# Strassen forms for the gate projection's sixth unit and for the attention half's up-projection, doubled products beside plain units, and x loaded by GpSimd's queue

## The chip, the cores and the metric

One core of one Trainium2 chip runs the whole layer in one launch. The metric is device time in microseconds (us), the median of the runs. The kernel before took 2658.71 us, the median of 3 runs that lie between 2658.05 and 2658.91.

## The reference

The inputs are x, 512 tokens of 2048 features, per-layer embeddings p of 256 features, and the weights. All of it is float32.

```
h   = RMSNorm(x)
[u | v_sgu | q | k | v_att | g_a | g_b] = h @ W_in
y_a = u * (tril(W_s) v_norm + b)            # 8 groups, chunks of 128 tokens
y_b = stick_breaking_attention(q, k, v_att) # 8 heads of 128
x  += (sigmoid(g_a) * (y_a W_up_a) + sigmoid(g_b) * (y_b W_up_b)) @ W_o
x  += SwiGLU(RMSNorm(x))                    # hidden size 5632
x  += sigmoid(RMSNorm(x) @ W_pg) * (p @ W_ple)
```

Here u and v_sgu go through GELU, and q, k and v_sgu have an RMSNorm over each group of 128. W_in has 9216 columns, of which g_a and g_b are 2048 each.

## The kernel before, in words

**Precision.** A float32 operand is split into a high part, which TensorE takes as fp32r, and the low rest. A product is three matmuls, high by high, high by low and low by high (`mm3`, L296 to L298).

**Units and pairs.** Everything is transposed: features on the partitions, tokens along the row. One output tile is a *pair*, 256 output features by 512 tokens. It is summed over *units*, each of 256 inputs by 256 outputs. A *plain* unit ("P") is four blocks of weights with three matmuls of 512 columns each, 12 in all. A *Strassen* unit ("S") needs seven products of half the columns (`PRODUCTS`), 21 matmuls of 256 columns. A product can be *doubled* (L692): its high weights meet high and low of the other operand in one matmul of 512 columns, with one matmul of 256 for the low weights. With `doubled=5` an S unit has 16 matmuls, with 7 it has 14. A doubled product holds a PSUM bank of its own until VectorE and ScalarE have added its halves (`mix_doubled`, L751). There are six banks in the pool "ps" and two in the pool "small"; y and z are the names of the two banks that the last two products, and all plain units, sum into. A pair that mixes S and P units is not doubled.

**Forms.** The operand that isn't weights is kept as *forms*: high and low blocks, four for a plain form, seven for S. A form that comes late starts as a plain one, with part of its blocks, and gets its other blocks by a second load of its source (`late_form`). The tables `..._UNTIL` say for how many of the first pairs each unit is used plain.

**Weights.** SyncE (SP) issues the loads of the weights in a planned order (L339 for P, L341 and L343 for S). For S, GpSimd (POOL) adds two blocks to two others on their way by an accumulating DMA (L363), which waits until the base has landed and stands in order with GpSimd's other work. ScalarE then writes the high parts `whi` (L359), VectorE two sums (L375) and the low parts `wlo` (L356), into three slots. There are four landing buffers.

**Order of work.** PE works through the pairs in a written order, and between units a clock ticks. `after(n, fn)` puts a step n ticks later, and `beside(steps)` runs a generator step by step, where `yield n` waits n ticks. `finish_waiting()` runs all that still waits at once.

**Stages in order.** First the embedding product (`ple_pair`), while x's eight tiles are loaded (`load_x`, L899). Then the projection with `w_in`: three plain pairs, whose weights are named `w_first`, and 33 more; the pairs of g_a and g_b are spilled to DRAM (`gsp`). Four pairs "s" feed the spatial gating in `sgu_v`: it transposes a tile on PE (L1029), norms it (ScalarE's L1052 with `rr`, which GpSimd works out at L928), and multiplies with W_s on PE (L1214, into the bank `mp`). The up-projection has 16 pairs of four plain units, in the order b, a for each j (b is the attention half with y_b, which was spilled; a the gating half with y_a). With each comes a reload of the gate, its scaling by the norm's row (`scaled`, L1224), the sigmoid and the merge. Then w_o (S, seven doubled), FFN in (S, seven doubled), FFN out in three passes, and the gate projection with eight pairs of five S units and three P units, undoubled. In its last pair `finish` (L1457 to L1469) closes pieces of the output as they come ready.

## Time and profile before

| what | us |
|---|---|
| median of 3 runs | 2658.71 |
| profiled execution, its own time | 2659.74 |
| its span | 2658.0 |
| PE busy (TensorE's matmuls) | 2638.2, 99% |
| VectorE busy | 2234.6, 84% |
| ScalarE busy | 1403.2, 53% |
| GpSimd busy | 448.1, 17% |

| stage, from the span's start | us |
|---|---|
| embedding product | 5.08 to 16.14 |
| first three projection pairs | 16.14 to 86.31 |
| the other 33 projection pairs | 86.31 to 815.28 |
| up-projection | 815.28 to 1004.59 |
| w_o | 1004.59 to 1165.98 |
| FFN in | 1165.98 to 2031.82 |
| FFN out | 2031.82 to 2481.78 |
| gate projection, and the end | 2481.78 to 2658.0 |

A stage begins with its first matmul. The records of the stages can be cut further at each pair's first matmul, which gives the price of one pair. A row of the view by windows lists a stretch (start:end), its length, then for PE, PE's weight loads, VectorE, ScalarE and GpSimd the busy time with the number of instructions, then the granted clock of TensorE (1.00 is full speed), the share of the DMA engines and GB/s. A row of the waits names an engine and its line, the engine and line that released it, the total wait, how often, and the longest. In a timeline, what stands in brackets is the idle time before an instruction and who ended it.

### The profile page before, as it was taken

The page shows a single profiled execution, that of the slowest core. Times are in us where ns is not written, and L with a number is a line of the kernel's source. Part 1 is how long each engine was busy: PE and PEld are TensorE (multiplying, and loading weights), DVE is VectorE, ACT ScalarE, POOL GpSimd, SP SyncE. Part 2 cuts the span into 40 slices and gives each one's busy share as a digit, 9 for nine tenths or more (in the row PEclk, how much of TensorE's full clock was granted, in tenths as well). Part 3 has the DMA queues.
Part 4 walks back from the last instruction along what each step waited for, and adds up shares of the span by engine and source line. Part 5 has one row for each costly group of instructions (what it writes and reads, how often), then busy time and mean ns, then how long its engine had stood idle before and what let it go on. Part 6 is the DMA issues. An engine that isn't in the chain of part 4 may idle for free.

```text
span 2658.0 us, 42554 instructions
## 1 busy us (share of the span) xinstructions
PE 2638.2 (99%) x15336; PEld 2312.3 (87%) x15336; DVE 2234.6 (84%) x3821; ACT 1403.2 (53%) x2233; POOL 448.1 (17%) x556
## 2 busy tenths in 40 slices
PE   8999999999999999999999999999999999999999
PEld 7888888888998888888888888888888888889898
DVE  8687878787886558999888888888889989989876
ACT  7756565655554334566444444444445445455543
POOL 0122222232220001101111111111110211211110
PEclk9999999999999999999999999999999999999999
DMA  7677777777775668978888888788887989978884
GB/s 229 162 194 171 192 173 191 172 191 179 178 191 183 232 212 268 265 236 218 223 210 216 206 200 203 194 209 204 199 207 221 257 227 273 229 229 260 256 240 123
DMA packets 293459, 559.77 MB, mean 211 GB/s; under 512 B 26368, under 2 KB 140544, under 8 KB 293248
## 3 DMA queue, kind: packets, MB, share of 16 engines
q1 hardware_dynamic: 231136, 441.95, 50.7%
q0 software_dynamic: 62112, 115.11, 27.5%
q8 instruction: 120, 1.97, 0.3%
q14 instruction: 91, 0.75, 0.1%
HBM read 505.57 MB, written 51.38 MB: 210 GB/s over the span
## 4 chain that ended last, share of the span: by engine, by line
PE 90%; DVE 4%; DMA 3%; issue 1%; ACT 1%; SPq 0%; POOL 0%; ACTq 0%; POOLq 0%; DVEq 0%
PE ps L692 53%; PE ps L298 10%; PE ps L297 9%; PE ps L296 9%; PE small L692 6%; DVE wlo L356 1%; DVE wholes L527 1%; DMA wholes<-w_ffn_out 1%; PE small L1103 1%; PE small L1155 1%; DVE parts L287 1%; PE small L1029 1%; DMA x<-wholes 1%; ACT whi L359 0%; PE small L1214 0%
## 5 line engine op out<-in xcount | busy, mean ns | idle before, releaser
L692 PE MATMUL ps<-parts,whi 128*128 128x512 f32 x4200 | 1409.4, 398 | 1.6 <-DVE out L796 1.0
L359 ACT ACTIVATE whi<-wholes 128x512 fp32r<-128x512 f32 (+2 forms) x940 | 871.5, 941 | 745.8 <-DVE wholes L375 286.6
L356 DVE TENSOR_TENSOR wlo<-wholes,whi 128x512 fp32r<-128x512 f32 (+2 forms) x940 | 979.4, 1076 | 73.7 <-ACT whi L359 73.0
L692 PEld LDWEIGHTS ps<-parts,wlo 128*128 128x128 f32 x4200 | 790.2, 188 | 178.2 <-issue 1.9
L692 PE MATMUL ps<-parts,wlo 128*128 128x256 f32 x4200 | 831.3, 279 | 0.9 <-DVE wlo L356 0.9
L692 PEld LDWEIGHTS ps<-parts,whi 128*128 128x128 f32 x4200 | 677.1, 189 | 10.5 <-issue 3.6
L297 PE MATMUL ps<-parts,whi 128*128 128x256 f32 (+1 forms) x1832 | 605.0, 331 | 0.7 <-DVE parts L287 0.5
L298 PE MATMUL ps<-parts,wlo 128*128 128x256 f32 (+1 forms) x1832 | 604.9, 331 | 0.5 <-DVE wlo L356 0.5
L296 PE MATMUL ps<-parts,whi 128*128 128x256 f32 (+1 forms) x1816 | 597.3, 330 | 7.4 <-ACT parts L286 5.3
L297 PEld LDWEIGHTS ps<-parts,whi 128*128 128x128 f32 x1832 | 347.0, 189 | 39.0 <-DVE parts L287 2.7
L296 PEld LDWEIGHTS ps<-parts,whi 128*128 128x128 f32 x1816 | 343.6, 190 | 40.4 <-ACT parts L286 5.7
L298 PEld LDWEIGHTS ps<-parts,wlo 128*128 128x128 f32 x1832 | 347.3, 190 | 32.4 <-DVE wlo L356 1.6
L375 DVE TENSOR_TENSOR wholes<-wholes 128x256 f32<-128x256 f32 (+1 forms) x820 | 345.0, 421 | 17.9 <-DVE wlo L356 1.4
L751 DVE TENSOR_TENSOR out<-out,ps 128x256 f32<-128x256 f32 x490 | 202.3, 416 | 147.6 <-ACT out L748 147.4
L363 POOL DMA_DIRECT2D wholes<-w_ffn_in x169 | 147.1, 870 | 702.1 <-DVE wholes L375 251.7
L363 POOL DMA_DIRECT2D wholes<-w_in x132 | 116.6, 885 | 531.3 <-DVE wholes L375 132.8
L692 PE MATMUL small<-parts,whi 128*128 128x512 f32 x480 | 190.3, 397 | 0.0
L287 DVE TENSOR_TENSOR parts<-wholes,parts 128x1024 fp32r<-128x1024 f32 (+3 forms) x137 | 122.8, 907 | 18.5 <-ACT parts L286 18.5
L286 ACT ACTIVATE parts<-wholes 128x1024 fp32r<-128x1024 f32 (+3 forms) x137 | 106.5, 800 | 54.2 <-DVE wholes L527 35.7
L748 ACT ACTIVATE out<-ps 128x256 f32<-128x256 f32 x258 | 96.3, 383 | 50.7 <-PE ps L692 46.7
L363 POOL DMA_DIRECT2D wholes<-w_ffn_out x64 | 55.7, 871 | 360.6 <-DMA wholes<-w_ffn_out 89.2
L1402 ACT ACTIVATE out<-out 128x512 f32<-128x512 f32 x44 | 27.9, 633 | 155.6 <-DVE out L1401 155.6
(124 smaller groups left out, 1770.0 us busy)
## 6 DMA issues: line engine op xcount, KB each, us to landing
wholes<-w_ffn_in SPq DMA_DIRECT2D x169, 384.0 KB, 5.5
wholes<-w_in SPq DMA_DIRECT2D x132, 384.0 KB, 5.1
wholes<-w_ffn_in SPq DMA_DIRECT2D x169, 256.0 KB, 4.7
wholes<-w_ffn_in POOLq DMA_DIRECT2D x169, 256.0 KB, 5.3
wholes<-w_in SPq DMA_DIRECT2D x132, 256.0 KB, 4.3
wholes<-w_in POOLq DMA_DIRECT2D x132, 256.0 KB, 5.0
wholes<-w_ffn_out SPq DMA_DIRECT2D x64, 384.0 KB, 6.3
wholes<-x SPq DMA_DIRECT2D x45, 512.0 KB, 5.8
```

The source lines that it names most:

```text
L286: return (nc.scalar.activation(hi, src, AF.Copy), nc.vector.tensor_tensor(out=lo, in0=src, in1=hi.bitcast(F32), op=ALU.subtract))
L287: nc.vector.tensor_tensor(out=lo, in0=src, in1=hi.bitcast(F32), op=ALU.subtract))
L296: nc.tensor.matmul(ps, sh, mh, start=start, stop=False)
L297: nc.tensor.matmul(ps, sh, ml, start=False, stop=False)
L298: return nc.tensor.matmul(ps, sl, mh, start=False, stop=stop)
L356: in_turn(nc.vector.tensor_tensor(out=self.lo[:, blocks], in0=r, in1=h.bitcast(F32), op=ALU.subtract))
L359: in_turn(nc.scalar.activation(h, r, AF.Copy))
L363: nc.gpsimd.dma_start(out=raw[:, 3:5], in_=self.src[:, 1:3], accum_op=ALU.add)
L375: in_turn(nc.vector.tensor_tensor(out=o, in0=x, in1=y, op=ALU.add))
L692: m = nc.tensor.matmul(out, l, r, start=first and k == 0, stop=last and k == 1)
L748: in_turn(nc.scalar.activation(out, x, AF.Copy, scale=scale))
L751: in_turn(nc.vector.tensor_tensor(out=out, in0=x, in1=y, op=op))
```

## The change

Four things change.

1. **Gate projection.** `GATE` goes from five S and three P units to six and two; the sixth is S from j = 2 on. All its pairs get `doubled=5` although they still hold plain units: five products take five "ps" banks, y takes the sixth, and z goes to a "small" bank. The plain units then start the bank z themselves.
2. **Up-projection of the attention half.** The four units of `w_up_b` become S, undoubled, with late forms for y_b: none at j = 0, two at j = 1, all four from j = 2 on, 26 unit uses in all. For j = 0 the order becomes a, b.
3. **Start.** x's tiles from the third on are issued by GpSimd instead of SP, p's first half by ScalarE, and ScalarE's table load comes behind that.
4. **Around the gating and the up-projection.** `sgu_v` waits three ticks rather than two before W_s's matmuls. `finish_waiting()` between projection and up-projection goes; what waits is carried over. The scaling of the 16 gates by the norm's row moves into the projection, two ticks after each gate pair and ahead of its spill; the sigmoid comes two ticks after its load rather than one.

The diff:

```diff
@@ -30,11 +30,12 @@
 EPS = 1e-6
 MASKED = -1e4
 
+UP_UNTIL = 1, 1, 2, 2
 PASSES = "SSSSSSSS", "SSSSSSSS", "SSSSPP"
 HALF = 1, 1, 1, 1, 2, 2, 2, 2
 PLAIN_UNTIL = HALF, HALF, (2, 2, 2, 2, 1, 1)
-GATE = "SSSSSPPP"
-GATE_UNTIL = 1, 1, 2, 2, 2, 1, 1, 1
+GATE = "SSSSSSPP"
+GATE_UNTIL = 1, 1, 2, 2, 2, 2, 1, 1
 PLACE = 7 * 256
 LATER = 3
 FFN_UNTIL = 1, 1, 2, 2, 2, 2, 2, 2
@@ -611,8 +612,10 @@
                     src, far)
 
     def plain_form(src, ready=always, gain=None, raw=1024, how="low", far=False):
+        hows = [how] * 2 if isinstance(how, str) else how
+
         def steps(form):
-            hi, lo = form.blocks = parts.take(1024, how), parts.take(1024, how)
+            hi, lo = form.blocks = [parts.take(1024, h) for h in hows]
             w = form.raw()
             if gain:
                 gained(hi.own(), w.f(), *gain)
@@ -629,7 +632,7 @@
             return tuple([x.own(0, T), x.own(T)] for x in form.blocks)
             yield
 
-        return Form("P", steps, [(parts, 1024, how)] * 2 + [(wholes, raw, "low")] * bool(raw),
+        return Form("P", steps, [(parts, 1024, h) for h in hows] + [(wholes, raw, "low")] * bool(raw),
                     ready, src, far)
 
     class Pair:
@@ -643,12 +646,13 @@
             self.n = {k: kinds.count(k) for k in "SP"}
             self.left = dict(self.n)
             self.both = all(self.n.values())
-            self.doubled = 0 if self.n["P"] else doubled
+            self.doubled = 0 if self.n["P"] and doubled > 5 else doubled
             self.o, self.home, self.banks = None, home, {}
 
         def at(self, name):
             if name not in self.banks:
-                self.banks[name] = small_bank() if name == len(PRODUCTS) - 1 else bank()
+                small = "z" if self.both and self.doubled else len(PRODUCTS) - 1
+                self.banks[name] = small_bank() if name == small else bank()
             return self.banks[name]
 
         def ends(self):
@@ -666,10 +670,11 @@
                     for ps, bs in zip(self.ends(), ((3, 2), (1, 0))):
                         for k, b in enumerate(bs):
                             first = start and u + k == 0
+                            fresh = not self.both or (self.doubled > 0 and b < 2)
 
                             mark(mm3(ps, wh[:, b], wl[:, b], xh[k], xl[k],
-                                     first and not self.both, stop and u == n - 1 and k == 1,
-                                     first and self.both and b < 2))
+                                     first and fresh, stop and u == n - 1 and k == 1,
+                                     first and not fresh and b < 2))
                     if prepare and u == 0:
                         prepare_late()
                     tick()
@@ -777,7 +782,8 @@
                 tt(c12, c12, p3[1], add)
             else:
                 yield
-                tt(o[:, :T], self.at("y"), o[:, :T], sub)
+                if not self.both:
+                    tt(o[:, :T], self.at("y"), o[:, :T], sub)
             yield
 
         def out(self, o=None):
@@ -842,11 +848,10 @@
             for u, ((xh, xl), (wh, wl)) in enumerate(ws):
                 for k, i in enumerate(bs):
                     mm3(ps, wh[:, i], wl[:, i], xh[k][:, a:b], xl[k][:, a:b],
-                        c + a > T and u + k == 0, k == 1 and u == len(ws) - 1)
+                        c + a >= T + (p.doubled == 0) and u + k == 0, k == 1 and u == len(ws) - 1)
             done(p.o, c + a, c + b, ps)
 
 
-    nc.scalar.preload_act_table_set("natural_log_exp_and_others")
 
     more_landings(4)
     for i in range(3):
@@ -858,11 +863,13 @@
     ple_spill = {}
     ps_p = []
 
-    def ple_operands():
+    def ple_operands(queue=None):
         raw = take(1024, "old")
         ps_p.extend(parts.take(1024, "high") for _ in range(2))
         for k in (0, T):
-            nc.sync.dma_start(out=raw.f(k, k + T), in_=pT[:, k : k + T])
+            (queue or nc.sync).dma_start(out=raw.f(k, k + T), in_=pT[:, k : k + T])
+            queue = None
+        for k in (0, T):
             split_into(*(x.own(k, k + T) for x in ps_p), raw.f(k, k + T))
         give(raw)
 
@@ -896,10 +903,12 @@
 
     def load_x():
         x_raw.append(take(1024, "old"))
-        nc.sync.dma_start(out=x_raw[-1].f(), in_=xT[len(x_raw) - 1])
+        queue = nc.gpsimd if len(x_raw) > 2 else nc.sync
+        queue.dma_start(out=x_raw[-1].f(), in_=xT[len(x_raw) - 1])
 
     w_ple_0 = plain_weights(w_ple[0])
-    ple_operands()
+    ple_operands(nc.scalar)
+    nc.scalar.preload_act_table_set("natural_log_exp_and_others")
     ple_pair(0, w_ple_0)
     load_x()
     gcol = consts.tile([P, ng], F32, name="gcol")
@@ -1207,7 +1216,7 @@
             rr = power(ssq, NT)
             yield 1
             times(gv, ps, rr)
-            yield 2
+            yield 3
             mp = small_bank()
             for t in range(NT):
                 s = slice(t * P, (t + 1) * P)
@@ -1218,6 +1227,10 @@
                 scalar=gcol[:, g_sgu + g : g_sgu + g + 1],
                 in1=bb.unsqueeze(1).to_broadcast([P, NT, P]),
                 op0=ALU.mult, op1=ALU.add)
+        if rnd == 3:
+            assert ("b", 3) in y_done
+            give(*att.values())
+            att.clear()
 
     def scaled(o, row):
         b = o.rearrange("p (b t) -> p b t", t=T)
@@ -1273,8 +1286,9 @@
 
     def plan_rest():
         for j in range(KU):
-            for b in "ba":
-                plan((w_up_a if b == "a" else w_up_b)[j], "PPPP")
+            for b in "ba" if j else "ab":
+                plan((w_up_a if b == "a" else w_up_b)[j],
+                     "PPPP" if b == "a" else now("SSSS", UP_UNTIL, j))
             if 0 < j < 6:
                 planned.append((w_ple[j + 2].rearrange("p (b c) -> p b c", b=4), 1, "P"))
         for j in range(KU):
@@ -1290,11 +1304,14 @@
             plan(w_gate[j], now(GATE, GATE_UNTIL, j))
 
     def y_form(c, i):
-        return plain_form((lambda: y_a[i]) if c == "a" else lambda: load(y_spill[i]),
-                          lambda: len(y_done) == 8, raw=0 if c == "a" else 1024,
-                          far=c == "b")
-
-    ys = {(c, i): y_form(c, i) for c in "ba" for i in range(4)}
+        def ready():
+            return len(y_done) == 8
+
+        if c == "a":
+            return plain_form(lambda: y_a[i], ready, raw=0, how="low" if i else ("high", "low"))
+        return late_form(lambda size=1024: load(y_spill[i], size), ready, far=True)
+
+    ys = {(c, i): y_form(c, i) for c in "ab" for i in range(4)}
     build(ys.values())
     for n, ((w, i), pr) in enumerate(zip(order, made())):
         if n == 0:
@@ -1323,11 +1340,14 @@
             nc.vector.tensor_tensor(out=y_a[i].f(), in0=o, in1=y_a[i].f(), op=ALU.mult)
             y_done["a", i] = True
         else:
-            d = tc.dram_tile([P, 1024], F32, name=nm("gsp"))
-            nc.sync.dma_start(out=d, in_=o)
-            gate_spill[w, i] = d
-    finish_waiting()
-    give(*att.values())
+            d = gate_spill[w, i] = tc.dram_tile([P, 1024], F32, name=nm("gsp"))
+
+            def spill_gate(o=o, d=d):
+                scaled(o, row1)
+                nc.sync.dma_start(out=d, in_=o)
+
+            after(2, spill_gate)
+    after(3, lambda: give(norm1.block))
 
 
     part = {}
@@ -1348,19 +1368,18 @@
     ms = [spilled_form("S", "mix", j) for j in range(KU)]
     build(ms)
     for j in range(KU):
-        for b in "ba":
+        for b in "ba" if j else "ab":
             s = load(gate_spill[b, j], 1024, "low")
             g = s.f()
-
-            def gate(g=g):
-                scaled(g, row1)
-                nc.scalar.activation(g, g, AF.Sigmoid)
-
-            after(1, gate)
-            pr = pair([ys[b, i] for i in range(4)], last=j == KU - 1)
-            for h, ps in zip((g[:, :T], g[:, T:]), pr.ends()):
-                nc.vector.tensor_tensor(out=h, in0=h, in1=ps, op=ALU.mult)
-            if b == "b":
+            after(2, lambda g=g: nc.scalar.activation(g, g, AF.Sigmoid))
+            pr = pair([ys[b, i] for i in range(4)], last=j == KU - 1, j=j,
+                      until=UP_UNTIL if b == "b" else None)
+            if pr.n["S"]:
+                tt(g, g, pr.out(), ALU.mult)
+            else:
+                for h, ps in zip((g[:, :T], g[:, T:]), pr.ends()):
+                    tt(h, h, ps, ALU.mult)
+            if j not in part:
                 part[j] = s
             else:
                 nc.vector.tensor_tensor(out=g, in0=g, in1=part[j].f(), op=ALU.add)
@@ -1372,8 +1391,6 @@
             ple_pair(j + 2)
             if j == 5:
                 ple_done()
-    give(norm1.block)
-
 
     norm2 = Norm()
     fs = [spilled_form("S", "x1", j, (g_ffn, j)) for j in range(KU)]
@@ -1476,9 +1493,9 @@
         if j:
             after(LATER, rest)
         if j == KU - 1:
-            pair(gs, j=j, until=GATE_UNTIL, parts_done=finish)
+            pair(gs, j=j, until=GATE_UNTIL, parts_done=finish, doubled=5)
         else:
-            o = pair(gs, j=j, until=GATE_UNTIL).out()
+            o = pair(gs, j=j, until=GATE_UNTIL, doubled=5).out()
             if j:
                 close(o)
             else:
```

What the change moves, at three places. First SP's queue at the start of the program (`ple` are stores of the embedding product, `w_first` the weights of the first three projection pairs, `xT` the tiles of x). Before:

```order
L339 DMA wholes<-w_first 128x512
L899 DMA wholes<-xT 128x1024 x2
L884 DMA ple_110<-out_91 128x1024
L339 DMA wholes<-w_first 128x512
L884 DMA ple_157<-out_140 128x1024
L899 DMA wholes<-xT 128x1024
L884 DMA ple_179<-out_162 128x1024
L339 DMA wholes<-w_first 128x512 x3
```

Now:

```order
L340 DMA wholes<-w_first 128x512
L907 DMA wholes<-xT 128x1024
L340 DMA wholes<-w_first 128x512 x3
L891 DMA ple_110<-out_91 128x1024
L340 DMA wholes<-w_first 128x512
L891 DMA ple_157<-out_140 128x1024
L340 DMA wholes<-w_first 128x512
L891 DMA ple_179<-out_162 128x1024
L342 DMA wholes<-w_in 128x2x256 x2
```

Three more loads of `w_first` stand ahead of the first store, whose source is only there when the first embedding pair is done. GpSimd's queue, now, at the same place:

```order
masks.py:197 MEMSET ident 128x128
L907 DMA wholes<-xT 128x1024
masks.py:199 ISA
masks.py:199 AFFINE_SELECT ident<-ident 128x128
L924 AFFINE_SELECT tri<-ones 128x128
L907 DMA wholes<-xT 128x1024
L364 DMA wholes<-w_in 128x512 x2
L907 DMA wholes<-xT 128x1024
```

Before, none of the rows on `xT` stood there; the third tile of x is now the second thing that GpSimd does in the program.

Second PE in a late pair of the gate projection, where its last S unit ends and the next plain unit begins (`ps_...` and `small_...` are banks of PSUM, `whi` and `wlo` weights). Before:

```order
L298 MATMUL ps_23817<-parts,wlo_81 128x256
L296 MATMUL ps_23824<-parts,whi_80 128x256
L297 MATMUL ps_23824<-parts,whi_80 128x256
L298 MATMUL ps_23824<-parts,wlo_81 128x256
...
L296 MATMUL ps_23824<-parts,whi_78 128x512
L297 MATMUL ps_23824<-parts,whi_78 128x512
L298 MATMUL ps_23824<-parts,wlo_79 128x512
```

Now:

```order
L697 MATMUL ps_24014<-parts,whi_75 128x512
L697 MATMUL ps_24014<-parts,wlo_76 128x256 x2
L697 MATMUL ps_24014<-parts,whi_75 128x512
L297 MATMUL ps_24019<-parts,whi_75 128x256
L298 MATMUL ps_24019<-parts,whi_75 128x256
L299 MATMUL ps_24019<-parts,wlo_76 128x256
...
L299 MATMUL ps_24019<-parts,wlo_80 128x512
L297 MATMUL small_24128<-parts,whi_79 128x512
L298 MATMUL small_24128<-parts,whi_79 128x512
L299 MATMUL small_24128<-parts,wlo_80 128x512
```

The products ahead of y are doubled now, and the plain units sum into y's bank and into a small bank.

Third PE around W_s's matmuls of the spatial gating (L1214 before, L1223 now). Before:

```order
L297 MATMUL ps_6402<-parts,whi_78 128x256
L298 MATMUL ps_6402<-parts,wlo_79 128x256
L1214 MATMUL small_6515<-wholes 128x128 x4
L692 MATMUL ps_6368<-parts,whi_76 128x512
L692 MATMUL ps_6368<-parts,wlo_77 128x256 x2
```

Now:

```order
L299 MATMUL ps_6416<-parts,wlo_78 128x256
L697 MATMUL ps_6382<-parts,whi_75 128x512
L697 MATMUL ps_6382<-parts,wlo_76 128x256 x2
...
L697 MATMUL ps_6403<-parts,whi_75 128x512
L697 MATMUL ps_6403<-parts,wlo_76 128x256 x2
L697 MATMUL ps_6403<-parts,whi_75 128x512
L1223 MATMUL small_6565<-wholes 128x128 x4
```

One group of doubled products, which stood behind W_s's four matmuls, now stands ahead of them.

## The prediction

> **What bounds the kernel now.** I read the page's busy times first, then PE's waits, then windows cut at the first matmul of each pair.
>
> ```profile
> PE 2638.2 (99%) x15336; PEld 2312.3 (87%) x15336; DVE 2234.6 (84%) x3821; ACT 1403.2 (53%) x2233; POOL 448.1 (17%) x556
> ```
>
> PE is busy for 2638.2 of 2658.0 us. So there are two ways to a shorter time: fewer columns through PE, or fewer of the some 20 us in which it is idle. The waits of PE (engine and line, who released it, total, times, longest) show the second:
>
> ```profile
> PE small L1214 <- ACT wholes L1052: 2.2, 1, 2.2
> PE ps L296 <- ACT whi L359: 2.1, 2, 1.9
> PE ps L692 <- DVE out L796: 1.0, 2, 0.8
> ```
>
> None is large, and all but the 1.0 lie at places that the change touches. The rest of the idle time is the head and the tail of the program.
>
> **The price of a unit.** Windows of five pairs: an up-projection pair (four plain units), w_o's second (four plain, four S undoubled), a late gate pair (five S undoubled, three plain), a projection pair of eight S doubled five times, and an FFN pair doubled seven times.
>
> ```profile
> 887.63:898.51 10.88, 10.88 (x50) 9.02 (x49) 6.23 (x7) 3.96 (x6) 0.00 (x0) 1.00 0.64 223
> 1026.35:1047.36 21.01, 21.01 (x134) 19.14 (x133) 19.31 (x35) 12.71 (x16) 2.65 (x3) 1.00 0.89 263
> 2548.26:2569.07 20.81, 20.81 (x143) 19.41 (x142) 15.23 (x24) 8.59 (x11) 3.00 (x3) 1.00 0.84 226
> 602.88:622.66 19.78, 19.78 (x130) 17.97 (x129) 15.63 (x27) 8.72 (x13) 3.49 (x4) 1.00 0.84 215
> 1270.28:1289.81 19.53, 19.53 (x114) 17.05 (x112) 17.30 (x32) 9.37 (x14) 4.33 (x5) 1.00 0.93 229
> ```
>
> PE's busy time equals the length in each, so these are prices of work. Plain: 10.88 / 4 = 2.72. S undoubled: (21.01 - 10.88) / 4 = 2.53, and from the gate pair (20.81 - 3 x 2.72) / 5 = 2.53 again. S doubled five times: 19.78 / 8 = 2.47.
>
> **Up-projection.** 26 unit uses go from 2.72 to 2.53: 26 x 0.19 = **-4.9**. What each b pair adds on other engines (S weights by accumulating DMA, VectorE's two sums and more low parts, the mixing) is about half of what eight S units need in the 602.88 row: 15.6 / 2 = 7.8 us of VectorE and 8.7 / 2 = 4.4 of ScalarE in a pair of 10.12, so PE's work hides it; without that cover it would cost the excess. The second halves of y_b's forms must be there for j = 1, about 11 us after j = 0's start; the w_o pair above does the same in its row without idle PE. Bound: nothing to 1.5, the idle time of w_o's third pair here, whose two waits for L796 are the 1.0 above:
>
> ```profile
> 1047.36:1069.83 22.47, 21.50 (x122) 18.27 (x121) 19.75 (x35) 11.67 (x16) 3.82 (x5) 1.00 0.98 283
> ```
>
> (22.47 against 21.01.) I take nothing, since the nearer row (1026.35) has no wait. The scaling of the gates moves from here into the projection: 16 x 1.22 us of VectorE, where it is busy for 15.63 of 19.78, so it fits. The DMA that spills each gate moves behind it by two ticks; its reload comes hundreds of us later.
>
> **Gate projection.** Six unit uses go from 2.72 to 2.47, 6 x 0.25 = -1.5, and the 32 S uses that exist (2 at j = 1, 5 at j = 2 to 7) get doubled, 32 x 0.06 = -1.8: **-3.3**. VectorE's share rises: from 15.23 by one S unit's share of the 602.88 row (15.63 / 8 = 1.95, less a plain unit's 6.23 / 4 = 1.56) and by the mixing of five doubled banks, at most the difference between FFN's 17.30 and 15.23: some 17.8 of 20.3. FFN's 17.30 of 19.53 is the same share, and PE waits for nothing there. In the last pair the end is set by y:
>
> ```profile
> 2648.41 0.69 DVE L1457 TENSOR_TENSOR out<-ps,out 128x512 f32<-128x512 f32 x1 [2.46 <-PE ps L298]
> ...
> 2653.73 1.45 DVE L1469 TENSOR_TENSOR out<-out,wholes 128x256 f32<-128x256 f32 x3
> ```
>
> From y's last matmul VectorE runs a chain to 2655.18. Behind y's last product stood 36 matmuls of 256 columns; now there are 24, so y ends 12 x 0.12 later relative to the pair's end and, with the pair 0.5 shorter, 0.8 later than before, with less work behind it. I give back 0.6 of the gain, bounds 0 and 0.8: **-2.7**.
>
> **The gating's wait.** The pair in which PE waited, then the stretches around the wait, and the chain of waits through it:
>
> ```profile
> 622.66:648.20 25.54, 23.31 (x146) 21.13 (x145) 18.01 (x31) 13.73 (x27) 4.91 (x6) 0.93 0.68 158
> ...
> 637.80:640.57 2.77, 0.54 (x5) 0.33 (x3) 0.00 (x0) 0.67 (x3) 1.94 (x2) 1.00 0.86 210
> 640.57:643.98 3.41, 3.41 (x15) 3.12 (x15) 0.78 (x2) 2.01 (x4) 0.92 (x1) 0.50 0.75 115
> ```
>
> ```profile
> 631.78 5.48 DMA wholes<-w_in
> ...
> 637.93 0.86 POOL wholes L363
> 638.79 1.08 POOL rr L928
> 639.87 0.02 issue
> 639.90 0.38 ACT wholes L1052
> 640.27 0.04 issue
> 640.32 1.69 PE small L1214 x7
> ```
>
> The small `rr` stood on GpSimd behind an accumulating DMA that waited for a load of weights, ScalarE's L1052 for `rr`, and PE for that: 2.2 us idle, then 3.41 us at a clock of 0.50. The pair took 25.54, where its neighbour with the same extra work took 21.43:
>
> ```profile
> 581.45:602.88 21.43, 21.43 (x135) 18.92 (x133) 15.99 (x27) 9.27 (x14) 3.48 (x4) 1.00 0.79 222
> ```
>
> So the place costs 4.1. The changed order puts eight products of 512 columns and as many of 256 between: 8 x 0.227 + 8 x 0.12 = 2.7 us more work ahead of W_s's matmuls, against 2.2 idle. It is enough by 0.5, and the clock isn't lowered: **-3.9**, bounds 0 and -4.2.
>
> The Trainium skill, page "TensorE: Matmul & The Clock Gate", section "HAM oscillation — how this bites in real kernels", tells to leave no gap on PE over some 3.4 us. The trace differs: 2.2 us were followed by a row at 0.50. By the page alone only the 2.2 of idle time would come back, and the sum below would be 1.7 smaller in its gain; the measurement decides.
>
> **Entry of the up-projection.** Its first two pairs, of the same plain units:
>
> ```profile
> 815.28:826.85 11.57, 11.35 (x51) 8.76 (x49) 8.95 (x13) 7.37 (x8) 0.00 (x0) 1.00 0.76 232
> 826.85:838.67 11.82, 11.29 (x49) 9.04 (x50) 10.59 (x11) 6.97 (x8) 0.00 (x0) 1.00 0.46 151
> ```
>
> They take (11.57 + 11.82) - 2 x 10.88 = 1.63 too long, while VectorE is at 10.59 of 11.82. The flush of all waiting steps goes, so do the scalings, and y_a's forms (which need no reload) come first. **-1.3** of the 1.63; bounds 0 and -1.63.
>
> **Start.** The chain, SP's issues, and the wait of PE at the second unit of the projection:
>
> ```profile
> 2.65 5.62 DMA gcol<-gains
> ...
> 8.36 1.34 ACT wholes L522 x2
> 9.70 0.53 ACT whi L359
> 10.23 0.04 issue
> 10.27 0.51 PE ps L296
> ```
>
> ```profile
> 14.66 0.38 SPq L899 DMA_DIRECT2D wholes<-xT  x1
> 17.17 0.33 SPq L884 DMA_DIRECT2D ple<-out  x1
> 17.55 1.78 SPq L339 DMA_DIRECT2D wholes<-w_first  x3
> ```
>
> ```profile
> 23.65 0.51 PE L296 MATMUL ps<-parts,whi 128*128 128x512 f32 x1 [1.90 <-ACT whi L359]
> ```
>
> SP is in order, so the loads of `w_first` stood behind stores that wait for results; now they are issued some 10 us earlier, and PE's wait goes. Against that, GpSimd issues x's third tile at about 1 us, ahead of `gcol`, the first x and the first weights, with 512 KB. At the rate of the first 50 us
>
> ```profile
> 0.00:50.00 50.00, 42.81 (x174) 33.46 (x175) 38.15 (x69) 42.06 (x62) 4.61 (x11) 1.00 0.87 269
> ```
>
> that is 524 KB / 269 GB/s = 1.95 us, if all of it goes first. An estimate with nearly all: the matmul of 10.27 at 12.07, and four plain units later 12.07 + 4 x 2.72 = 22.95 in place of 23.65: **-0.7**. Bounds: -2.3, if the tile costs nothing, and +1.85, if the wait at 23.65 also stays. I take -0.7, since the DMA engines are busy for 0.87 here and can't give a tile away.
>
> The Trainium skill, page "DMA: Bandwidth & Descriptors", section "Queues, rings and completion order", has each DMA engine take turns between queues packet by packet. That speaks against a second queue here: the third tile would share with the weights and `gcol` rather than stand behind them. No row before has two queues loading at the start. By it the start is worth -0.7 rather than -2.3, and the sum stays as it is.
>
> **Sum.** -4.9 - 2.7 - 3.9 - 1.3 - 0.7 = -13.5. The profiled execution's own 2659.74 becomes 2646.2. The median of the runs stands 1.03 below that execution, so **2645**.
>
> **Rivals.** First, *a wait that moves*: the gating's wait, which comes from a load of weights, appears at another of the eight places, since GpSimd and the landings get more S units. 3.9 is given back: 2649. For it: `rr` still shares GpSimd's queue with L363. Against: its cause was one late landing among eight such places. Second, *the start gets worse*: +1.85 instead of -0.7, 2648 at least; for it, the share of 0.87. Third, *S saves nothing in the up-projection*, the change not doing what it says: 4.9 lost, 2650. Against it stand the two rows that both give 2.53.
>
> Fourth, on the other side, *banks in the gate projection*. Its pairs now take all six "ps" banks, so the next pair's first product waits until VectorE has read the oldest. The price per pair lies between the 1.5 of w_o's third pair, where L692 waits for just such a reading, and the 4.1 of a stall with a lowered clock; there are six pairs that follow a fully doubled one. At 4.1: +25, 2670. It decides from (13.5 / 6) = 2.3 us per pair on. Against it: the five doubled banks are last written two plain units, 5.4 us, before the pair's end, and y isn't needed until five products into the next pair, 3.5 us; FFN with seven such banks and no plain units between shows no wait at all.
>
> **How the numbers follow.** The forecast 0.58, the moved wait 0.18, the worse start 0.12, S without gain 0.05, banks 0.07. The range goes up to 2653, which takes in the first three rivals with the two largest bounds left on top (2650, 1.5 for the late forms and 1.3 for the entry), and down to 2639: 2645 less 1.6 more at the start, 0.3 and 0.3 more at the two waits, 0.6 at the tail, and the rest of some 3 for waits of a few tenths that vanish with them. A measurement here can tell about 0.2%, 5.3 us, from no change: faster means below 2653.4. Faster 0.86, the same 0.07 (two of the first three rivals together), slower 0.07 (the banks).
>
> **What would show it.** Late gate pairs of 20.3 in place of 20.81, b pairs of 10.1 in place of 10.88, and no row below a clock of 1.00 around the gating, whose pair takes 21.4; the first two up pairs at 10.9; the second unit's matmul at about 22.9. VectorE in the gate near 88%. It would be wrong if L697 waits for VectorE in the gate, if L1223 keeps a wait, or if the first matmuls come later than 12.1.

## The result and the profile after

The changed kernel takes 2666.88 us, the median of 7 runs (2664.36 to 2670.45), against 2658.71 of the kernel before (2657.06 to 2662.34). The ratio is 1.0029 with an interval of 1.0020 to 1.0038: slower by 0.3%, where 2645 and faster was forecast. The profiled execution took 2665.25 us with a span of 2663.1, 5.1 more than before. The medians part by 8.2 and the profiles by 5.1: the profiled execution lies 1.6 below the median of its kernel here, and 1.0 above it before. What follows is about the 5.1.

The page's busy times:

```profile
PE 2635.2 (99%) x15423; PEld 2310.9 (87%) x15423; DVE 2297.3 (86%) x3950; ACT 1426.0 (54%) x2278; POOL 447.9 (17%) x575
```

PE's busy time fell by 3.0 us only, and the span rose. A busy time counts a matmul under a lowered clock at its full length (in the lowered stretch from 887.5 on, matmuls of 256 columns start 0.21 us apart, behind it 0.12), so part of what the fewer columns saved was spent that way. The waits of PE name what is new (engine and line, who released it, total, times, longest; L297 to L299 are `mm3`, L357 and L360 the low and high parts of the weights, L288 the low parts of forms):

```profile
PE ps L297 <- ACT parts L287: 5.8, 1, 5.8
PE ps L298 <- DVE parts L288: 4.0, 3, 2.1
PE ps L299 <- DVE wlo L357: 3.8, 4, 1.2
PE ps L297 <- ACT whi L360: 2.0, 1, 2.0
PE small L950 <- DVE diag L948: 1.3, 2, 0.7
PE small L1223 <- ACT wholes L1061: 1.1, 1, 1.1
```

The first is the head of the program, which is there before too. Of the next three, 9.8 us in all, 8.4 lie in the up-projection and in w_o, and one of 1.2 at 30.44, in the first projection pairs. Cut at the same matmuls as before, the stages compare so (two pairs between the gating and the up-projection, 39.58 us in both, are left out):

| stage | before, us | after, us | difference | forecast |
|---|---|---|---|---|
| start of the program to the first of the 33 pairs | 86.31 | 85.61 | -0.7 | -0.7 |
| projection up to the gating | 536.35 | 538.51 | +2.2 | 0 |
| the seven pairs from the gating's wait on | 153.04 | 152.04 | -1.0 | -3.9 |
| up-projection | 189.31 | 191.78 | +2.5 | -6.2 |
| w_o | 161.39 | 165.91 | +4.5 | 0 |
| FFN in, FFN out | 1315.80 | 1314.92 | -0.9 | 0 |
| gate, seven pairs | 149.73 | 147.56 | -2.2 | -2.8 |
| last pair and end | 26.53 | 27.14 | +0.6 | +0.1 |

(The last two rows of the forecast make up its -2.7; the entry's -1.3 is in that of the up-projection.) Of the 18.6 us between the forecast of -13.5 and the 5.1 found, 13.2 lie in the up-projection and w_o.

**What came as forecast.** An up-projection pair with four S units, one of the late gate pairs, and the first two pairs of the up-projection:

```profile
861.66:871.74 10.08, 10.08 (x86) 10.08 (x85) 9.98 (x16) 6.28 (x9) 0.00 (x0) 1.00 0.44 114
```

```profile
2554.79:2575.07 20.28, 20.28 (x121) 17.97 (x120) 17.55 (x28) 9.04 (x12) 3.05 (x4) 1.00 0.85 240
```

```profile
815.74:826.64 10.90, 10.90 (x50) 9.01 (x49) 10.87 (x15) 5.01 (x6) 0.00 (x0) 1.00 0.95 292
826.64:837.52 10.88, 10.88 (x49) 9.01 (x48) 9.49 (x18) 8.81 (x12) 0.00 (x0) 1.00 0.72 265
```

10.08 was forecast as 10.1, and 20.28 as 20.3 with VectorE at 17.55 (17.8). The entry took 21.8 in place of 23.4.

**Where the up-projection lost.** The embedding product after pair a of j = 2, pair b of j = 3 and pair b of j = 4 (2.72, 10.1 and 10.1 without waits):

```profile
882.64:887.48 4.84, 2.89 (x14) 2.07 (x12) 1.40 (x3) 2.27 (x3) 0.00 (x0) 1.00 0.38 95
887.48:901.28 13.80, 13.07 (x84) 12.78 (x85) 10.04 (x12) 5.83 (x8) 0.88 (x1) 0.75 0.52 172
915.17:926.98 11.81, 10.70 (x85) 10.30 (x86) 10.05 (x12) 5.84 (x8) 0.00 (x0) 1.00 0.45 120
```

These three are 7.6 us too long; in the second, PE runs for 6.83 us at half clock behind two waits. The chain of waits through the place, then ScalarE's timeline and SP's issues ahead of it:

```profile
872.51 12.62 DMA wholes<-gsp
...
885.21 0.04 ACT wholes L1374
...
886.17 1.26 ACT whi L360
```

```profile
876.00 1.06 ACT L1374 ACTIVATE wholes<-wholes 128x1024 f32<-128x1024 f32 x1 [5.63 <-DMA wholes<-gsp]
876.97 0.61 ACT L360 ACTIVATE whi<-wholes 128x512 fp32r<-128x512 f32 x1
885.21 1.06 ACT L1374 ACTIVATE wholes<-wholes 128x1024 f32<-128x1024 f32 x1 [7.62 <-DMA wholes<-gsp]
```

```profile
867.82 0.38 SPq L891 DMA_DIRECT2D ple<-out  x1
868.25 0.73 SPq L519 DMA_DIRECT2D wholes<-gsp  x1
869.08 0.86 SPq L342 DMA_DIRECT2D wholes<-w_up_b  x1
870.00 1.18 SPq L344 DMA_DIRECT2D wholes<-w_up_b  x1
871.27 0.40 SPq L519 DMA_DIRECT2D wholes<-mix  x1
871.76 0.45 SPq L340 DMA_DIRECT2D wholes<-w_up_a  x1
872.51 0.33 SPq L519 DMA_DIRECT2D wholes<-gsp  x1
```

The gate for the next pair is the last of a burst. It is on its way for 12.62 us, and ScalarE, which is in order, stands at its sigmoid (L1374) for 7.62 of them with the high parts of the weights (L360) behind it. Four windows of two us in this stretch show that the DMA engines are full meanwhile and empty afterwards (the last two columns are their share and GB/s):

```profile
872.00:874.00 2.00, 2.00 (x10) 1.66 (x9) 1.14 (x3) 0.00 (x0) 0.84 (x1) 1.00 1.02 416
878.00:880.00 2.00, 2.00 (x11) 1.65 (x10) 0.31 (x1) 0.00 (x0) 0.88 (x1) 1.00 1.05 301
...
884.00:886.00 2.00, 1.52 (x7) 0.94 (x5) 0.01 (x1) 0.79 (x1) 0.00 (x0) 1.00 0.29 74
886.00:888.00 2.00, 0.52 (x2) 0.50 (x2) 0.54 (x1) 2.00 (x4) 0.00 (x0) 0.88 0.01 4
```

The same place in the kernel before (from 866.8 to 882, where the changed kernel's rows run from 866.8 to 886), its DMA packets and its two gates with their median time from issue to landing, then the changed kernel's:

```profile
DMA packets 1304, 4.75 MB, mean 313 GB/s; under 512 B 144, under 2 KB 144, under 8 KB 1304
wholes<-gsp SPq DMA_DIRECT2D x2, 512.0 KB, 8.0
```

```profile
DMA packets 2068, 5.28 MB, mean 275 GB/s; under 512 B 207, under 2 KB 719, under 8 KB 2067
wholes<-gsp SPq DMA_DIRECT2D x2, 512.0 KB, 10.1
```

So there are some more bytes, and they come in smaller pieces and at a lower rate. Which of these makes the gate late was not tried.

**Where w_o lost.** Its first two pairs were 21.76 and 21.01 before:

```profile
1007.52:1031.66 24.14, 22.07 (x97) 17.94 (x96) 17.12 (x22) 9.92 (x11) 2.61 (x3) 1.00 0.94 318
1031.66:1056.30 24.64, 22.87 (x135) 20.70 (x133) 23.78 (x45) 13.87 (x17) 3.48 (x4) 0.93 0.96 283
```

PE waits for forms of w_o (L288) that VectorE makes late, 2.1 and 1.8 us. Ahead of w_o's first matmul, 8 loads of `mix` were issued, where it had been 10.

### The profile page after: what moved, and what is told of

It is laid out like the page before. It is cut to its first block, busy times and chain, and to the rows that moved or that the text cites. A ratio compares the mean times of both kernels' runs of the same rounds, so it can differ in the third digit from the quotient of the medians.

```text
span 2663.1 us, 42994 instructions
## 1 busy us (share of the span) xinstructions
PE 2635.2 (99%) x15423; PEld 2310.9 (87%) x15423; DVE 2297.3 (86%) x3950; ACT 1426.0 (54%) x2278; POOL 447.9 (17%) x575
## 4 chain that ended last, share of the span: by engine, by line
PE 79%; DVE 8%; DMA 8%; issue 2%; ACT 2%; POOL 0%; SPq 0%; ACTq 0%; DVEq 0%; POOLq 0%
PE ps L697 55%; PE small L697 6%; PE ps L299 5%; PE ps L298 5%; PE ps L297 5%; DVE wlo L357 3%; DVE wholes L528 1%; DMA wholes<-gsp 1%; DMA wholes<-w_ffn_out 1%; DMA wholes<-w_up_b 1%; DVE parts L288 1%; DVE out L756 1%; PE small L1164 1%; DVE wholes L376 1%; DMA wholes<-mix 1%
## 5 line engine op out<-in xcount | busy, mean ns | idle before, releaser
L697 PE MATMUL ps<-parts,whi 128*128 128x512 f32 x4390 | 1468.6, 397 | 1.1 <-DVE out L756 0.7
L360 ACT ACTIVATE whi<-wholes 128x512 fp32r<-128x512 f32 (+2 forms) x947 | 883.8, 947 | 702.4 <-DVE wholes L376 314.8
L357 DVE TENSOR_TENSOR wlo<-wholes,whi 128x512 fp32r<-128x512 f32 (+2 forms) x947 | 991.1, 1082 | 56.7 <-ACT whi L360 55.8
L697 PE MATMUL ps<-parts,wlo 128*128 128x256 f32 x4390 | 868.2, 279 | 0.1
L697 PEld LDWEIGHTS ps<-parts,whi 128*128 128x128 f32 x4390 | 707.1, 189 | 8.7 <-issue 2.2
L298 PE MATMUL ps<-parts,whi 128*128 128x256 f32 (+1 forms) x1700 | 552.7, 325 | 4.1 <-DVE parts L288 4.0
L299 PE MATMUL ps<-parts,wlo 128*128 128x256 f32 (+1 forms) x1700 | 552.5, 326 | 3.8 <-DVE wlo L357 3.8
L297 PE MATMUL ps<-parts,whi 128*128 128x256 f32 (+1 forms) x1689 | 547.2, 325 | 7.9 <-ACT parts L287 5.8
L376 DVE TENSOR_TENSOR wholes<-wholes 128x256 f32<-128x256 f32 x846 | 356.6, 421 | 24.5 <-DMA wholes<-w_up_b 7.2
L298 PEld LDWEIGHTS ps<-parts,whi 128*128 128x128 f32 x1700 | 323.9, 191 | 37.3 <-DVE parts L288 6.1
L756 DVE TENSOR_TENSOR out<-out,ps 128x256 f32<-128x256 f32 x525 | 216.6, 415 | 158.6 <-ACT out L753 158.4
L297 PEld LDWEIGHTS ps<-parts,whi 128*128 128x128 f32 x1689 | 321.4, 191 | 34.6 <-ACT parts L287 6.2
L299 PEld LDWEIGHTS ps<-parts,wlo 128*128 128x128 f32 x1700 | 324.0, 191 | 30.7 <-DVE wlo L357 5.4
L287 ACT ACTIVATE parts<-wholes 128x256 fp32r<-128x256 f32 (+3 forms) x145 | 111.6, 795 | 42.5 <-DVE wholes L528 37.2
L288 DVE TENSOR_TENSOR parts<-wholes,parts 128x1024 fp32r<-128x1024 f32 (+3 forms) x145 | 128.6, 900 | 3.0 <-ACT parts L287 2.8
```

What stands on the lines that cost most here:

```text
L287: return (nc.scalar.activation(hi, src, AF.Copy), nc.vector.tensor_tensor(out=lo, in0=src, in1=hi.bitcast(F32), op=ALU.subtract))
L288: nc.vector.tensor_tensor(out=lo, in0=src, in1=hi.bitcast(F32), op=ALU.subtract))
L297: nc.tensor.matmul(ps, sh, mh, start=start, stop=False)
L298: nc.tensor.matmul(ps, sh, ml, start=False, stop=False)
L299: return nc.tensor.matmul(ps, sl, mh, start=False, stop=stop)
L357: in_turn(nc.vector.tensor_tensor(out=self.lo[:, blocks], in0=r, in1=h.bitcast(F32), op=ALU.subtract))
```

## The experiments

The runs of one kernel spread by some 8 us, so the ratios decide only where their intervals part, and the lengths of single pairs in the profiles say where time went. The theory to begin with (A): S units in the up-projection make the burst at a pair's start longer, ScalarE stands at the late gate, and w_o's forms are pushed back. Its rival (B): the edits around it cost, the moved scaling, the later sigmoid, the missing flush.

**Plain units in the up-projection, the rest of the change kept.**

```diff
-                     "PPPP" if b == "a" else now("SSSS", UP_UNTIL, j))
+                     "PPPP")
...
-        return late_form(lambda size=1024: load(y_spill[i], size), ready, far=True)
+        return plain_form(lambda: load(y_spill[i]), ready, far=True)
```

> The changed kernel, but the attention half's up-projection keeps plain units and plain forms for y_b (order a, b at j = 0, moved scaling and later sigmoid stay). Theory A (S units there bring 896 KB instead of 512 KB per unit and crowd the reloads of gates and mix, on which ScalarE and the weights behind it wait): the up-projection falls from 191.8 to about 187.7 us, w_o from 165.9 to 161.4, and the time from 2666.9 to about 2658. Rival B (the moved scaling, the later sigmoid and the lacking flush are what costs): up-projection and w_o stay at 190 and 166, and the time goes up by the 4.9 that S saves, to 2670 or so.

Measured: 2660.98 us, ratio 1.0001 (0.9992 to 1.0010). The up-projection took 187.71 as A says, w_o 163.88 rather than 161.4: its first two pairs were 21.76 and 21.01 again, and two later pairs were 2.4 and 1.5 us longer than 19.5, with 2.1 us of waiting for VectorE at one line (L802, the reading of banks); the kernel before is 1.5 over 19.5 in the first of them, with 1.0 of such waits. ScalarE's wait for the gate, first in the change, then here:

```profile
ACT wholes L1374 <- DMA wholes<-gsp: 66.5, 13, 8.0
```

```profile
ACT wholes L1374 <- DMA wholes<-gsp: 22.0, 11, 3.8
```

B falls: with its edits in place, the up-projection is 1.6 shorter than before. The S units with their forms turn 1.0001 into 1.0029.

**The gate projection alone, on the kernel before** (the tables `GATE` and `GATE_UNTIL`, `doubled=5`, and the bank for z).

> The kernel before with the gate projection's part alone (sixth S unit, five products doubled). Theory A: late gate pairs of 20.28 in place of 20.81, some 2.8 us less in the stage, about 1.3 of it given back at the end: -1.5 in all. Rival (six ps banks make PE wait): pairs of 20.8 or more, and a time of 2659 or above.

Measured: 2657.34, ratio 0.9988 (0.9979 to 0.9997), faster by a little. Late pairs of 20.28 (the six pairs between the first and the last take 122.65 to 122.96 in every profile with this edit, 125.48 without it), and the end as in the change:

```profile
2632.41:2659.70 27.29, 20.59 (x133) 18.54 (x131) 17.72 (x31) 6.93 (x11) 0.00 (x0) 0.93 0.10 39
```

From its first matmul to the end of the span the last pair takes 27.3 us, where it took 26.5. The rival on banks falls. The first gate pair, with a norm in it, took 28.01 in this profile, with a wait of 2.0 and a lowered clock; it took 24.25 to 25.78 with the code of before and 24.14 to 25.95 in the others with this edit, so that pair varies from profile to profile.

**One tick more at the gating alone, on the kernel before.**

```diff
             times(gv, ps, rr)
-            yield 2
+            yield 3
```

> The kernel before, only W_s's matmuls one tick later (three ticks for two). If the wait was simply cured: the pair of 25.54 falls to about 21.1, the seven pairs from there from 153.1 to 149, time -3.9. If the wait moves to other places of the same eight (GpSimd's small power behind the accumulating DMA, a bank read late): the seven pairs sum to 151.5 to 152.5, and the time falls by 1 or less.

Measured: 2662.64, ratio 1.0012 (1.0003 to 1.0021), slower. The two pairs in question:

```profile
622.08:643.16 21.08, 21.08 (x142) 19.23 (x141) 16.02 (x28) 13.05 (x27) 4.63 (x5) 1.00 0.76 180
643.16:670.51 27.35, 24.41 (x154) 22.05 (x153) 19.39 (x34) 13.84 (x38) 6.67 (x8) 0.94 0.67 153
```

The first is cured (25.54 before) and the second has the wait, with its lowered clock (22.41 before). The chain is the old one at a new place:

```profile
650.92 5.24 DMA wholes<-w_in
...
656.83 0.88 POOL wholes L363
657.71 1.07 POOL rr L928
```

The seven pairs sum to 153.9, 0.9 more than before: the wait moved and nothing was won.

**The start alone, on the kernel before** (x from the third tile on by GpSimd's queue, p's first half and the table load by ScalarE).

> The kernel before with x from the third tile on by GpSimd's queue, p's first half by ScalarE's, and ScalarE's table load behind it. If the start is what the changed trace shows: 0.7 us less at the 34th... that is at the first of the 33 projection pairs (85.6 in place of 86.31) and no stall later. Rival (what the projection loses before the gating, some 2.1 us between 86 and 604, comes from x's loads): those pairs are longer here too, and the pair that began at 602.88 begins later than 603.

Measured: 2659.51, ratio 0.9998 (0.9989 to 1.0008). The first of the 33 pairs began at 86.89, 0.6 later than before and not 0.7 earlier (over all profiles, 85.61 to 87.99 in the twelve that have this part and 85.52 to 86.50 in the four that don't); from there to 623.35 it was 536.46, as before (536.35). So the projection's 2.2 don't come from x's loads, and no gain of the start stands out from what varies from profile to profile.

**The gates' sigmoid ahead of the spill, on the change.**

```diff
                 scaled(o, row1)
+                nc.scalar.activation(o, o, AF.Sigmoid)
                 nc.sync.dma_start(out=d, in_=o)
...
-            after(2, lambda g=g: nc.scalar.activation(g, g, AF.Sigmoid))
```

> The changed kernel, with the gates' sigmoid applied in the projection, ahead of the spill, so that ScalarE has nothing to wait for at a gate's reload. Theory A1 (S in the up-projection makes the reload take some 12 us, ScalarE stands at the sigmoid for it, and the high weights behind it come late for PE): ScalarE's 66.5 us of waiting for the reload go, the pair of 13.81, the embedding product of 4.83 and the pair of 11.80 fall to about 10.1, 2.7 and 10.1, the up-projection from 191.8 to some 184.5, the time from 2666.9 to about 2660; w_o stays near 165. Rival (the weights themselves land late, since S brings 896 KB a unit): the same pairs stay long, and the time within 2 of 2666.9.

Measured: 2735.42, ratio 1.0284 (1.0270 to 1.0298). The projection grew by 76 us between its first pair and the gating: between attention's logarithms and exponentials the sigmoid makes ScalarE change its table, and over a hundred loads at 1283 ns stand in the profile. But the up-projection, which is what the run was for, fell from 191.78 to 183.90. Its weights came in the same burst, the second gate was again 12.63 us on its way, and the embedding product and the next pair b took

```profile
963.31:966.03 2.72, 2.72 (x13) 2.25 (x12) 2.72 (x4) 1.64 (x2) 0.00 (x0) 1.00 0.35 83
966.03:976.53 10.50, 10.42 (x85) 10.18 (x84) 9.88 (x15) 6.60 (x9) 0.00 (x0) 1.00 0.51 151
```

So ScalarE's place in the order is the link: with the same late gate, but without an instruction of ScalarE that waits for it, the loss of 7.9 us is gone. (The 16 sigmoids, 16.9 us of ScalarE's work, have left the stage too.) w_o still took 164.08, so its loss is another.

**Room for forms, plain units** (y_b's plain forms given the room of S forms in the first variant, the weights as there).

> The variant with plain units in the up-projection (up 187.7, w_o 163.9, 10 loads of mix issued before w_o's first matmul), with y_b's plain forms each given the room of an S form in the space for forms, and nothing else. Theory A2 (w_o's extra time with S units comes from room: y_b's S forms leave less for w_o's forms, so that their loads and building fall into w_o): about 7 loads of mix ahead of w_o, and w_o at 165 to 167. Rival (it comes from the bytes and the work that S brings): 10 loads, w_o 161.4 to 164.

Measured: 2661.44, ratio 1.0008 (0.9999 to 1.0018). 8 loads of `mix` ahead of w_o rather than 10, its first two pairs 22.73 and 22.85 (45.6 for 42.8), the whole of w_o 164.23. Room alone takes 2.8 of the 6.0 us in those two pairs; the whole stage is hardly longer than with plain units and no such room (163.88). The profiled execution took 2666.82, 5.4 above the median of this kernel, so its rows may not be typical.

**The gating's power by ScalarE, on the kernel before.**

```diff
-            rr = power(ssq, NT)
+            rr = rms_tile()[:, :NT]
+            nc.scalar.activation(ssq, ssq, AF.Ln)
+            nc.scalar.activation(rr, ssq, AF.Exp, scale=-0.5)
```

> The kernel before, with the spatial gating's small power worked out by ScalarE (logarithm and exponential, with changes of its function table) rather than by GpSimd. If GpSimd's order (the power behind an accumulating DMA that waits for weights) makes the wait: no wait for L1052 of 2 us and no lowered clock, the pair of 25.54 falls to about 21.4, the seven pairs from 153.0 to 149, time -4. Rival (ScalarE is late by its own queue or the table changes): waits of one or two us stay, the seven pairs 152 to 155.

Measured: 2661.22, ratio 1.0002 (0.9993 to 1.0011). The wait of 2.2 us and the lowered clock go, but three waits of up to 0.9 us come for it, and the seven pairs sum to 153.2. So the chain through GpSimd, as the traces show it, makes the one long wait, and the way by ScalarE is as long. One profile is thin evidence here: in that of the start alone, with GpSimd's power and two ticks, the wait was 1.2 and no clock was lowered there either.

**The sigmoid behind its pair, on the change.**

```diff
-            after(2, lambda g=g: nc.scalar.activation(g, g, AF.Sigmoid))
...
+            nc.scalar.activation(g, g, AF.Sigmoid)
             if pr.n["S"]:
```

> The changed kernel, with the gate's sigmoid put behind its pair (just ahead of the product that uses it) rather than two ticks into it, so that the weights' high parts don't stand behind it on ScalarE; no other edit. Theory A1 (ScalarE held by the gate's late reload): the long pair of 13.81 and the pair of 11.80 go to about 10.1, the up-projection from 191.8 to some 184, as it was with the sigmoid ahead of the spill; w_o 164 to 166; time 2666.9 - 7.5 = about 2659. Rival (moved to the pair's end, the sigmoid delays the reading of the banks and PE waits there): up-projection 187 or more, time 2662 or above.

Measured: 2669.97, ratio 1.0038 (1.0026 to 1.0050), where about 2659 was expected; up-projection 191.16. This run tells the two apart less than it was meant to: on ScalarE the sigmoid still stands ahead of the same high parts (it ran at 885.97, the high parts at 886.93), since none were split between the second tick and the pair's end. **The same with two ticks at the gating:**

> The one before it (sigmoid behind its pair), with W_s's matmuls after two ticks again. If the third tick only moves the gating's wait and costs 3 us in the runs, as it did alone (ratio 1.0012): 3 less than with three ticks, about 2656, with a wait for L1061 of 2 us at the first gating pair or none by luck. If the third tick helps here: 2662 or above.

Measured: 2663.63, ratio 1.0012 (1.0004 to 1.0021), up-projection 191.67, the seven pairs 150.45. With the sigmoid unmoved in effect, the pair of runs shows a cost of the third tick a second time, though of the 6.3 us between them only 2.3 lie in the seven pairs (152.77 with three ticks). The wait comes and goes by itself: the seven pairs take 150.45 to 153.68 in six profiles with two ticks, 152.05 to 154.05 in eight with three (those of the sigmoid ahead of the spill and of the power by ScalarE aside).

**Plain units in the up-projection and two ticks.**

> Plain units in the up-projection and two ticks at the gating, so what is left is the gate projection's part, the start and the entry of the up-projection. If the parts add up as measured alone (gate -3, entry -1.6, start 0): about 2655.5 to 2656.5, ratio 0.9983. If the loss of w_o seen with plain units (163.9 for 161.4) is a cost of its own: 2658.

Measured: 2657.57, ratio 0.9993 (0.9985 to 1.0002): less than half of what the parts promised (0.9983), and not told from no change. w_o took 161.71 here, so the 163.88 with plain units and three ticks is no fixed cost of the other edits.

**Two of y_b's units as S instead of four** (sigmoid behind its pair, two ticks).

```diff
-UP_UNTIL = 1, 1, 2, 2
+UP_UNTIL = 1, 1, 1, 1
...
-                     "PPPP" if b == "a" else now("SSSS", UP_UNTIL, j))
+                     "PPPP" if b == "a" else now("SSPP", UP_UNTIL, j))
...
+        if i > 1:
+            return plain_form(lambda: load(y_spill[i]), ready, far=True)
```

> Sigmoid behind its pair, two ticks, and only two of the four units of y_b as S from j = 1 on, 14 uses instead of 26. Theory (room and bytes for S forms push w_o's loads and building into w_o): gain in the up-projection 14 x 0.19 = 2.7 instead of 4.9, w_o between plain's 163.9 and 165.9, more loads of mix ahead of w_o than 7; the time equal to that with four S units or up to 2 less. Rival (w_o's loss doesn't depend on it): w_o 165 to 166, the time 2 above that with four S units.

Measured: 2652.16, ratio **0.9967** (0.9955 to 0.9979), faster than both kernels. Up-projection 185.28, w_o 160.41. Neither expectation holds: w_o lost nothing at all, and the time is 11.5 below that with four S units, not 2. **The same edit alone on the change** (sigmoid at the second tick, three ticks):

> The changed kernel with one edit: two of y_b's four units as S from j = 1 on, 14 uses instead of 26 (sigmoid two ticks into its pair and three ticks at the gating, as in the change). If the number of S units alone (their bytes in the burst of loads at a pair's start, and their room) is what the change lost by: b pairs of 10.53 with no wait, up-projection 185.3, w_o 160.4 to 162, time 2666.9 - 6.5 - 4.5 = about 2656. If the sigmoid's place was needed too: waits at the embedding products stay, up-projection 187 or more, time 2659 or above.

Measured: 2654.01, ratio 0.9981 (0.9972 to 0.9990). The embedding product and the pair that were 4.84 and 13.80, then w_o's first two pairs:

```profile
886.32:889.04 2.72, 2.72 (x14) 2.25 (x13) 2.69 (x5) 1.55 (x2) 0.00 (x0) 1.00 0.34 96
889.04:899.57 10.53, 10.53 (x69) 9.59 (x67) 5.67 (x8) 4.75 (x7) 0.87 (x1) 1.00 0.89 300
```

```profile
1004.26:1026.02 21.76, 21.76 (x97) 18.02 (x96) 18.37 (x26) 10.72 (x12) 1.74 (x2) 1.00 0.86 283
1026.02:1047.04 21.02, 21.02 (x135) 19.14 (x134) 20.95 (x39) 12.07 (x17) 2.63 (x3) 1.00 0.97 309
```

No wait is left in either stage's first pairs. ScalarE still waits 46.1 us for gates in all, but the longest single wait is 5.2 rather than 8.0, short enough that the high parts come in time. So the number of S units is what the change lost by, and with this smaller burst the order of ScalarE did no harm.

**Two runs on w_o**, of one time each (before it, the kernel before took 2663.39 on that chip). First two S units, with the other two forms given the room of S:

> Two S units of four as before, and the plain forms of the other two given the room of S forms, so that the forms fill as much as in the change and the weights bring the bytes of two S units. If room is the cause: w_o's first two pairs, 42.8 us with two S units, take 45.5 or more (48.8 in the change). If bytes are: 42.8 to 43.5. The up-projection stays at 185.3 in both.

Measured: 2654.67; first two pairs of w_o 21.76 and 21.01, up-projection 185.28. Room does nothing here. Then three S units:

> Three S units of four from j = 2 on (two at j = 1), a step between two and four in bytes and in room. Up-projection without waits would take 184.2. If the burst of loads is over its limit only with four: b pairs of 10.3 without wait and w_o's first two pairs below 44. If the loss grows evenly with each unit: waits of about 1 us at some embedding products and b pairs, up-projection 186 or more, w_o's first two pairs near 45.8.

Measured: 2662.00; no wait in the up-projection, b pairs of 10.33, 184.09 in all. That doesn't tell how large a burst may be, for the order of the loads is another here: the second gate is issued ahead of most of the pair's weights, and the longest that a gate is on its way is 7.1 us (12.6 in the change, 10.0 with two S units).

```profile
868.33 0.46 SPq L519 DMA_DIRECT2D wholes<-gsp  x1
870.21 0.38 SPq L342 DMA_DIRECT2D wholes<-w_up_b  x1
```

ScalarE waits 14.5 us for gates in all, less than with two S units (46.1) and with none (22.0). So the gate's place in the burst matters too, and the number of S units by itself doesn't put these waits in order. But w_o's first two pairs:

```profile
1000.17:1026.28 26.11, 23.11 (x98) 18.65 (x97) 19.54 (x31) 10.45 (x14) 2.66 (x3) 0.96 0.86 268
1026.28:1047.79 21.51, 21.51 (x135) 19.64 (x134) 19.41 (x38) 11.29 (x14) 2.61 (x3) 0.97 0.94 272
```

47.6, as bad as with four. What decides there stays open: plain units with full room lost 2.8, two S units with full room nothing, three S units 4.9. Neither room nor bytes puts these in order, nor does the number of `mix` loads issued ahead (8, 8 and 9). What is shown is only that the late thing is a form of w_o behind a reload of `mix`, that the loss is there in all five profiles with three or four S units (4.2 to 6.3 in those two pairs) and in none of the three with two, and that it stays when ScalarE's wait for the gate is gone.

## Why the prediction was wrong

- **Up-projection: wrong, and this is the step that failed.** The price of an S unit was right (10.08 a pair). What failed is "so PE's work hides it", and the scaling and the reloads costed at nothing. I compared the busy times of VectorE and ScalarE with the length of a pair, and never followed the loads at a pair's start. The S weights, with their accumulating DMAs, stand in one burst with the reload of the gate that ScalarE waits for; the row of the kernel before had the wait already (ScalarE idle for 44.8 us at this sigmoid, behind VectorE's scaling, which itself waited 20.5 us for the same loads). -6.2 was forecast, +2.5 came; without the wait it is 183.9, which is -5.4.
- **w_o: missing from the sum.** I took the row 1026.35 for a proof that late forms cost nothing. That row has behind it an up-projection of plain units; with three or four S units there, w_o's own late forms are no longer free. Nothing was taken for this stage, and +4.5 came; its mechanism stays open.
- **The gating: wrong.** "It is enough by 0.5" looked at one place of eight. The rival of a wait that moves was right, at 0.18, and in a stronger form: alone, the third tick costs 3 us in the runs and 0.9 in the profile. In the change, waits of 0.7 and 1.1 us lie in the pairs that follow, and the second is at L1223, which the prediction had named as a sign of being wrong. The price of 4.1 for the place was read from one trace; with the same two ticks the pair took 22.96 instead of 25.54 in the profile of the start alone.
- **Gate projection: right in mechanism**, -0.53 a pair, and the rival on banks didn't occur. (32 x 0.06 is 1.9, not 1.8.) The end was mis-sized: the last pair and the end take 0.6 more than before, where 0.1 was taken. VectorE's chain from y's last matmul begins 17.8 us into the last pair (16.9 before), later by 0.9, about the 0.8 of the forecast; but from there to the end it is 9.4 us, hardly less than the 9.6 before. So the pair's own gain of 0.55 was lost as well, and to give back 0.6 of the gain, with a bound of 0.8, was too little: 1.2 went.
- **Entry: right**, -1.6 for -1.3. **Start: -0.7 in the one trace, and by luck.** The first matmul came 0.7 us later (5.76 for 5.08; 5.67 to 6.05 in all profiles that have this part, 4.85 to 5.24 in those that don't), where 1.8 was taken for the matmul at 10.27, and the wait at 23.65 went, so that matmul came at 21.83 rather than the forecast 22.95. Then a wait of 1.2 at 30.44, for low parts behind a load of `w_first`, took most of it back. Alone it showed no gain. Which of the start's edits delays the first matmul was not tried by itself.
- **The projection's +2.2** was not foreseen. In the ten profiles with the moved scaling (the sigmoid ahead of the spill aside) it takes 537.0 to 538.5, in the five without 536.3 to 536.6; that the scaling causes it was not tried by itself.
- The rival on banks gave 2670, near the 2666.88 measured, but that is chance: no such wait occurred.

The clock went as in the trace before: the lowered stretches inside the kernel before, the change and the third tick alone follow waits of 2.2 (before), 2.0 and 1.8 (the change) and 2.3 us.

## What to carry to other kernels

When work on an engine gets cheaper by operands that cost more bytes, add up the loads that are issued together at one place, in order of issue, and see which in-order engine waits for the last of them and what is queued behind it; the mean DMA share (0.64 in such a pair) tells nothing of it. A dose is worth trying before the whole: two of four units gave more than four. And a wait that comes from the phase of two queues is not removed by shifting it one tick: look at all the places of its kind, and in more than one profile, since such a wait comes and goes.

## What was unexpected of the hardware

- A load of 512 KB that lands some 3.1 us after its issue in a quiet place (gates at 992.70 and 1000.96 in the changed kernel) takes 12.62 at the end of a burst that fills the DMA engines (share 0.93 to 1.07 from 872 to 884).
- In the changed kernel the clock fell to 0.50 for 3.41 us after a wait of 1.8 us (1038.55 to 1040.31), yet after one of 2.1 us at 1026.95, 12 us ahead of that, it did not fall.
- A change of ScalarE's function table took 1283 ns each time; 107 of them in the run with the sigmoid in the projection, where the kernel before has 5, came with 76 us more there.
